# GpSimd for the state-space weight tables and the recurrence over the chunks, in a two-layer recurrent decoder step

## Chip, cores and metric

One core of a Trainium2 chip. The time is that of one execution on the device, in microseconds (us), median of the runs shown.

## What is computed

One inference step of two layers on 256 tokens of a prompt and 8 samples of 4 tokens, 288 columns in all, width 2048, float32. Only layer 0 matters here. Its input projection feeds a diagonal state-space part (S5: 64 groups, each with a complex state of 64) and a gated linear attention (GLA: 4 heads); both meet in one output projection, and an MLP follows. Cut to what the change touches:

```
abar = exp(a * dt); bbar = (abar - 1) / a * b          # complex, per group
bu   = einsum('blgq,gpq->blgp', u, bbar)               # what each token adds to the state
x[t] = abar * x[t-1] + bu[t]                           # associative_scan over the tokens
y    = Re(einsum('blgp,gqp->blgq', x, c)) + d_skip * u # then gelu and a sigmoid gate
# GLA, per head and chunk: bcum = cumsum(log_a)
qd, kd = q * exp(bcum), k * exp(-bcum)
o = tril(qd kd^T) v + qd s;  s = exp(blast) s + (k exp(blast - bcum))^T v;  o = head_rmsnorm(o) * silu(g)
```

## The kernel before

**The stream.** Every large product takes its weights in granules of 512 rows by 256 columns. SyncE loads one (`load`, L174), ScalarE rounds it to `wh` (L187), VectorE makes the rest `wl = raw - wh` (L188), and TensorE multiplies the activations with both (`mm`, L202 to L204: three products of 288 columns for each 128 x 128 block, 24 a granule). ScalarE and VectorE work one to two granules ahead; `wh` and `wl` have four buffers each, two granules.

**Work between the granules.** All else is written as generators, which `go` and `start` put on a list with a rate. After each granule `pump` adds the rate to each one's account and takes a step of it for every whole 1.0; `until` yields until a flag is set, `need` and `finish` force steps up to a flag, and `defer` puts an instruction behind a later granule. This sets only the order in which each engine's instructions stand. Each engine then goes through its own queue in that order as soon as the semaphores that it waits for allow, and an instruction that waits holds up all that stand behind it on its engine. GpSimd's queue has memsets, transfers between HBM, DRAM buffers and SBUF, and so far no arithmetic.

**S5.** Tokens go in chunks of 4, 72 chunks; pairs of groups lie on the 128 partitions (32 pairs, in 8 tables q of 4 pairs).
- `s5_tables`: `powers(q)` makes a table of abar^(3-s) bbar into `tpre`, part of the tile `hr`, two buffers (q odd and even): eight VectorE instructions, L627, L628 and twice L631 for each of two parts, and copies on ScalarE (L633). `turn(q)`, a granule later, transposes it on TensorE (L643), and `adds(q)` multiplies with the tokens (L664) into the chunks' states `eh`. `pairs` (L713 to L717, VectorE) lets every second chunk take over the state of the one before.
- `s5_scan`: 31 rounds over the remaining chunks, each a chain of three VectorE instructions (L745, L747, L748) of 128, 64 and 64 elements; two rounds a step, at rate 1.2. `last` has the samples' final states.
- `s5_y`: copies the last state (`hlast`, L785), makes the output table of c abar^(t+1) for 4 pairs (`table(q)`: L776 to L778 on VectorE, then two deferred copies by ScalarE for each of two parts, L782, into `t3`, also in `hr`, two buffers), lets the rest of the chunks take over their states (`pairs`), and multiplies on TensorE: L798, and L801, which reads `eh` and `t3`. The table of q + 1 is issued in step q.

**GLA.** `gla_decays` makes the decays (VectorE and ScalarE, rate 0.6), waits for the flag `gqk`, which is set when q and k are there, and multiplies them into q and k (L987 to L990) for heads 0 and 1, then 2 and 3. `gla_head(h)` multiplies the scores (L1019), makes the states (L1052), reads the samples' states (L1060) and gives the output (L1077 to L1085); `gla_fin` sums the squares over partitions by a product with ones (L1135). GpSimd's queue has the transfers of the samples' states (L1005, four a head) and of each head's final state (L1053).

Of the kernel before, what the change touches and what calls it, by code (L numbers as in the profile page):

```python
# [15 lines left out]
T = 288          # tokens: 256 of the prompt, then 8 samples of 4  # L16
# [4 lines left out]
KG = 4           # k-tiles of a weight granule  # L21
# [5 lines left out]
# layout of the constants' array: name -> (first column, columns)  # L27
# [49 lines left out]
class Base:  # L77
# [62 lines left out]
    def finish(self, name=None):  # L140
        """Has the side work that gives a flag (or all of it) emit what is left up to that flag."""
# [164 lines left out]
        # vectors, as columns; those of the first norm ahead of the rest  # L306
# [20 lines left out]
    def x_parts(self):  # L327
        """x for the first layer's input projections: it comes in quarters of its columns, each ahead of a granule."""
# [39 lines left out]
    def spread_r(self):  # L368
        """The tokens' scales, on all partitions."""
# [19 lines left out]
    def load_h(self):  # L389
        """x again, transposed, as the residual stream."""  # L390
# [15 lines left out]
NJ = 32          # pairs of groups  # L406
NCH = 72         # chunks: 8 of the samples, then 64 of the prompt
# [8 lines left out]
class S5:  # L416
# [59 lines left out]
    def s5_loads2(self, i):  # L476
        """More of the loads; they are spread over the first products."""
# [18 lines left out]
    def s5_tables(self):  # L496
# [7 lines left out]
        # A-bar: the states of a pair of groups on the partitions  # L504
# [51 lines left out]
        # (A-bar - 1) / a  # L556
# [15 lines left out]
        # A^8  # L572
# [5 lines left out]
        # C, block-diagonal and transposed, its imaginary part negated; B-bar  # L578
# [20 lines left out]
        # initial states of the samples  # L599
# [18 lines left out]
        def powers(q):  # L618
            """A^(3-s) B-bar of 4 pairs, block-diagonal."""
# [34 lines left out]
        def adds(q):  # L654
            """What the chunks add to the states; the kernel."""
# [49 lines left out]
    def pairs(self, q, src, dst, n, t1, t2):  # L705
        """Every second of n chunks takes over the state that the chunk before it leaves (4 pairs of groups)."""
# [12 lines left out]
    def s5_scan(self):  # L719
        v = self.nc.vector  # L720
        eh = self.eh
        self.nc.gpsimd.memset(self.hr[:, 0:2048], 0.0)
# [5 lines left out]
        def last():  # L728
            """The samples' final states."""
# [14 lines left out]
        for c in range(10, 72, 2):  # L744
            v.tensor_mul(out=t1, in0=a, in1=eh[:, :, :, c].rearrange("p (o r) j -> p o r j", o=1).to_broadcast(sh))  # L745
            next(last, None)
            v.tensor_add(out=t2, in0=t1[:, 0], in1=t1[:, 1, ::-1])  # L747
            v.tensor_add(out=eh[:, :, :, c + 2], in0=eh[:, :, :, c + 2], in1=t2)  # L748
            if c % 4 == 2:
                yield  # L750
# [1119 lines left out]
```

## Time and profile before

| | |
|---|---|
| time, three runs | 2815.69, 2812.72, 2815.59 us; median 2815.59 |
| span of the profiled execution, first to last instruction | 2813.8 us |
| the median over that span | 1.8 us |
| TensorE busy | 2778.5 us (99%) |
| VectorE, ScalarE, GpSimd busy | 1728.4, 1344.3, 212.3 us (61, 48, 8%) |
| DMA | 511.86 MB, mean 182 GB/s |

The profiled execution's own time is not listed beside its span; what lies around the span is taken as the 1.8 us to the median. How to read it: a matmul's busy time overlaps the next one's, so TensorE's share tells where it pauses, not how near it is to its peak. With TensorE at 99%, the question for a change on other engines is which of TensorE's pauses it ends, which it makes, and at what clock TensorE runs. VectorE and ScalarE matter where TensorE waits for them. Line numbers in what follows are those of the kernel before, unless the order of the changed one is shown.

### The profile page before, as it was taken

What the parts mean: (1) busy time and instruction counts of PE and PEld (TensorE: products, weight loads), DVE (VectorE), ACT (ScalarE), POOL (GpSimd) and SP (SyncE); (2) the same over time, 40 slices, a digit from 0 to 9 for tenths busy, and PEclk for the clock granted to TensorE, in tenths of its full rate; (3) what the DMA queues carried; (4) which work ended last, traced back from release to release, by engine and by line L of the source; (5) the groups of instructions that cost most, each with busy time, mean ns of one, the idle gap of its engine ahead of it and who ended that gap; (6) DMA issues with size and microseconds to landing.
All of it is one profiled execution on the core that took longest, in us unless ns stands there. A gap on an engine that the chain in (4) does not pass through costs nothing.

```text
span 2813.8 us, 52593 instructions
## 1 busy us (share of the span) xinstructions
PE 2778.5 (99%) x20648; PEld 2688.8 (96%) x20648; DVE 1728.4 (61%) x3259; ACT 1344.3 (48%) x2459; POOL 212.3 (8%) x326
## 2 busy tenths in 40 slices
PE   8999999999999999999999999999999999999998
PEld 7988999999999999999988898889999999999998
DVE  7887668555555555556466665867655555555555
ACT  5646755544444444445433343445544444444445
POOL 3110112000000000000112222210000000000000
PEclk9999999999999999999999999999999999999999
DMA  7455567555555555555678878875555555555554
GB/s 210 130 155 140 161 195 228 160 167 165 165 164 165 163 168 164 166 164 146 197 223 250 269 249 271 266 254 173 164 166 164 166 165 165 164 167 163 167 165 131
DMA packets 449511, 511.86 MB, mean 182 GB/s; under 512 B 23282, under 2 KB 423052, under 8 KB 449232
## 3 DMA queue, kind: packets, MB, share of 16 engines
q1 hardware_dynamic: 414320, 412.67, 48.6%
q0 software_dynamic: 28096, 90.16, 10.1%
q10 hardware_dynamic: 6848, 5.68, 0.6%
q8 instruction: 162, 2.65, 0.4%
q14 instruction: 85, 0.70, 0.1%
HBM read 460.08 MB, written 47.56 MB: 180 GB/s over the span
## 4 chain that ended last, share of the span: by engine, by line
PE 94%; DVE 4%; ACT 1%; issue 1%; DMA 0%; ACTq 0%; DVEq 0%
PE g L202 29%; PE g L203 28%; PE g L204 28%; PE s L1551 1%; PE n L1545 1%; PE s L1500 1%; DVE wl L188 1%; PE n L801 1%; PE s L664 0%; PE s L1419 0%; ACT wh L187 0%; DVE hr L745 0%; PE n L798 0%; PE s L1490 0%; PE s L643 0%
## 5 line engine op out<-in xcount | busy, mean ns | idle before, releaser
L187 ACT ACTIVATE wh<-raw 128x512 fp32r<-128x512 f32 x1556 | 963.1, 629 | 1203.0 <-PE g L203 1153.7
L188 DVE TENSOR_TENSOR wl<-raw,wh 128x512 fp32r<-128x512 f32 x1556 | 1035.8, 688 | 664.3 <-ACT wh L187 652.2
L202 PE MATMUL g<-xh,wh 128*128 128x288 f32 x3856 | 1158.6, 300 | 3.0 <-DVE gy L938 1.4
L204 PE MATMUL g<-xh,wl 128*128 128x288 f32 x3856 | 1138.2, 295 | 3.8 <-DVE wl L188 3.7
L203 PE MATMUL g<-xl,wh 128*128 128x288 f32 x3856 | 1141.0, 296 | 0.0
L202 PEld LDWEIGHTS g<-xh,wh 128*128 128x128 f32 x3856 | 726.4, 188 | 14.4 <-issue 9.5
L204 PEld LDWEIGHTS g<-xh,wl 128*128 128x128 f32 x3856 | 728.9, 189 | 5.4 <-DVE wl L188 5.4
L203 PEld LDWEIGHTS g<-xl,wh 128*128 128x128 f32 x3856 | 727.4, 189 | 5.2 <-issue 3.3
L203 PE MATMUL g<-hl,wh 128*128 128x288 f32 x2048 | 606.2, 296 | 0.0
L204 PE MATMUL g<-hh,wl 128*128 128x288 f32 x2048 | 605.2, 296 | 0.0
L202 PE MATMUL g<-hh,wh 128*128 128x288 f32 x2048 | 604.7, 295 | 0.0
L202 PEld LDWEIGHTS g<-hh,wh 128*128 128x128 f32 x2048 | 389.1, 190 | 0.0
L204 PEld LDWEIGHTS g<-hh,wl 128*128 128x128 f32 x2048 | 384.0, 188 | 0.0
L203 PEld LDWEIGHTS g<-hl,wh 128*128 128x128 f32 x2048 | 383.8, 187 | 0.0
L1727 DVE TENSOR_TENSOR hr<-hr,g 128x288 f32<-128x288 f32 x256 | 116.3, 454 | 186.6 <-PE g L204 186.6
L1719 ACT ACTIVATE us<-sq 128x288 f32<-128x288 f32 x128 | 56.9, 445 | 146.2 <-DVE sq L1718 146.2
L1718 DVE SCALAR_TENSOR_TENSOR sq<-g,rbc 128x288 f32<-128x288 f32 x128 | 58.5, 458 | 94.5 <-PE g L204 94.3
L1553 DVE SCALAR_TENSOR_TENSOR cin<-cin,wps,s 128x512 f32<-128x512 f32 x128 | 89.7, 742 | 7.4 <-PE s L1551 6.7
L1523 POOL DMA_DIRECT2D cin<-in_state_mlstm_c_dram x64 | 45.3, 708 | 305.6 <-DMA out_sample_mlstm_c_dram<-cin 284.0
L1334 POOL DMA_DIRECT2D out_sample_mlstm_m_dram<-mo x1 | 0.6, 620 | 838.7 <-DVE mk L1338 838.7
L1720 ACT ACTIVATE hh<-us 128x288 fp32r<-128x288 f32 x128 | 57.0, 445 | 4.1
L203 PE MATMUL g<-yl,wh 128*128 128x288 f32 x192 | 56.7, 295 | 0.0
(504 smaller groups left out, 1928.9 us busy)
## 6 DMA issues: line engine op xcount, KB each, us to landing
raw<-in_w_mlp_up_dram SPq DMA_DIRECT2D x256, 512.0 KB, 3.7
raw<-in_w_mlp_down_dram SPq DMA_DIRECT2D x256, 512.0 KB, 3.6
raw<-in_w_in_odd_dram SPq DMA_DIRECT2D x128, 512.0 KB, 4.6
raw<-in_w_in_even_dram SPq DMA_DIRECT2D x64, 512.0 KB, 4.0
cin<-in_state_mlstm_c_dram POOLq DMA_DIRECT2D x64, 512.0 KB, 5.2
out_sample_mlstm_c_dram<-cin POOLq DMA_DIRECT2D x64, 512.0 KB, 5.5
raw<-in_w_out_even_dram SPq DMA_DIRECT2D x32, 512.0 KB, 4.4
raw<-in_w_out_odd_dram SPq DMA_DIRECT2D x32, 512.0 KB, 3.6
```

Of the source, the lines that this page charges most:

```text
L187: nc.scalar.activation(out=wh[:, 0:n], in_=src, func=AF.Copy)
L188: nc.vector.tensor_tensor(out=wl[:, 0:n], in0=src, in1=wh[:, 0:n].bitcast(F32), op=ALU.subtract)
L202: nc.tensor.matmul(g.ps[j], lhsT=wh, rhs=xh, start=opens and k == 0, stop=False)
L203: nc.tensor.matmul(g.ps[j], lhsT=wh, rhs=xl, start=False, stop=False)
L204: nc.tensor.matmul(g.ps[j], lhsT=wl, rhs=xh, start=False, stop=closes and k == n - 1)
L801: nc.tensor.matmul(ps[:, j, :], lhsT=t3[:, ri, j].rearrange("p t c -> p (t c)"), rhs=eh[:, ri, jj, 0:NCH], start=False, stop=ri == 1)
L1523: nc.gpsimd.dma_start(out=cin[g], in_=part(I["state_mlstm_c"], g))
L1553: v.scalar_tensor_tensor(out=t[:, b, :], in0=t[:, b, :], scalar=wp[:, c:c + 1], in1=pb, op0=ALU.mult, op1=ALU.add)
L1718: nc.vector.scalar_tensor_tensor(out=t, in0=ps, scalar=0.0, in1=self.rbc, op0=ALU.max, op1=ALU.mult)
L1719: nc.scalar.activation(out=sq, in_=t, func=AF.Square)
L1720: nc.scalar.activation(out=hh[:, j, :], in_=sq, func=AF.Copy)
L1727: nc.vector.tensor_add(out=self.h[:, j, :], in0=self.h[:, j, :], in1=ps)
```

## The change

`powers` and the recurrence of `s5_scan` go from VectorE to GpSimd, instruction by instruction. `powers(1)` is issued at once behind `powers(0)`, and from then each table one step earlier. The output table becomes a method and goes to GpSimd, where its last instruction writes both halves into `t3` directly; ScalarE's 32 copies go. Tables 0 and 1 are issued within the recurrence, behind its 13th and 23rd round, the others two steps ahead. The end of `gla_decays` becomes a generator of its own with rate 1.0, started when k is there. `gla_fin` yields once more before its product. Comments are left out here, and so are hunks that change only them.

```diff
         def powers(q):
...
-            t = [tp.tile(sh, F32, name=f"cm{i + 1}") for i in range(2)]
+            t = [tp.tile(sh, F32, name=f"pm{i + 1}") for i in range(2)]
+            gp = nc.gpsimd
             for ri in range(2):
-                v.tensor_mul(out=t[0], in0=a[0], in1=b[ri])
-                v.tensor_mul(out=t[1], in0=a[1], in1=b[1 - ri])
+                gp.tensor_mul(out=t[0], in0=a[0], in1=b[ri])
+                gp.tensor_mul(out=t[1], in0=a[1], in1=b[1 - ri])
                 for g in range(2):
                     gs = slice(64 * g, 64 * g + 64)
-                    v.tensor_tensor(out=tpre[gs, ri, :, 0:3, g, :], in0=t[0][gs], in1=t[1][gs],
-                                    op=ALU.subtract if ri == 0 else ALU.add)
+                    gp.tensor_tensor(out=tpre[gs, ri, :, 0:3, g, :], in0=t[0][gs], in1=t[1][gs],
+                                     op=ALU.subtract if ri == 0 else ALU.add)
...
         powers(0)
+        powers(1)
         yield
         for q in range(8):
             turn(q)
-            if q < 7:
-                powers(q + 1)
+            if q < 6:
+                powers(q + 2)
...
     def s5_scan(self):
...
-        self.nc.gpsimd.memset(self.hr[:, 0:2048], 0.0)
+        gp.memset(self.hr[:, 0:2048], 0.0)
+        for g in range(2):
+            gs = slice(64 * g, 64 * g + 64)
+            self.nc.scalar.activation(out=self.cc()[gs], in_=self.ct[gs, :, :, 16 * g:16 * g + 16], func=AF.Copy)
...
         for c in range(10, 72, 2):
-            v.tensor_mul(out=t1, in0=a, in1=eh[:, :, :, c].rearrange("p (o r) j -> p o r j", o=1).to_broadcast(sh))
+            gp.tensor_mul(out=t1, in0=a, in1=eh[:, :, :, c].rearrange("p (o r) j -> p o r j", o=1).to_broadcast(sh))
             next(last, None)
-            v.tensor_add(out=t2, in0=t1[:, 0], in1=t1[:, 1, ::-1])
-            v.tensor_add(out=eh[:, :, :, c + 2], in0=eh[:, :, :, c + 2], in1=t2)
+            gp.tensor_add(out=t2, in0=t1[:, 0], in1=t1[:, 1, ::-1])
+            gp.tensor_add(out=eh[:, :, :, c + 2], in0=eh[:, :, :, c + 2], in1=t2)
+            if c in (34, 54):
+                self.table(c // 54)
             if c % 4 == 2:
                 yield
...
+    def table(self, q):
...
+        for ri in range(2):
+            gp.tensor_mul(out=tm, in0=c3[ri], in1=a3[0])
+            gp.tensor_mul(out=m3, in0=c3[1 - ri], in1=a3[1])
+            for g in range(2):
+                gs = slice(64 * g, 64 * g + 64)
+                gp.tensor_tensor(out=t3[gs, ri, :, :, 16 * g:16 * g + 16], in0=tm[gs], in1=m3[gs],
+                                 op=ALU.add if ri == 0 else ALU.subtract)
...
     def s5_y(self):
...
-                v.tensor_mul(out=tm, in0=c3[ri], in1=a3[0])
-                v.tensor_mul(out=m3, in0=c3[1 - ri], in1=a3[1])
-                v.tensor_tensor(out=tm, in0=tm, in1=m3, op=ALU.add if ri == 0 else ALU.subtract)
-                for g in range(2):
-                    gs = slice(64 * g, 64 * g + 64)
-                    self.defer(lambda t=t3[gs, ri, :, :, 16 * g:16 * g + 16], s=tm[gs]:
-                               nc.scalar.activation(out=t, in_=s, func=AF.Copy))
...
-        table(0)
         self.pairs(0, 10, 11, 31, f[0], f[1])
...
+            if q < 6:
+                self.table(q + 2)
             if q < 7:
-                table(q + 1)
                 self.pairs(q + 1, 10, 11, 31, f[0], f[1])
...
         act.activation(out=cum, in_=cum, func=AF.Exp, scale=-1.0 / 16)
-        yield from self.until("gqk")
+        self.flags.add("dec")
+
+    def gla_decays2(self):
...
+        yield from self.until("dec")
         for h in (0, 2):
...
     def gla_fin(self, h, osb, acc, r):
         nc, v = self.nc, self.nc.vector
+        yield
...
-        self.start(self.gla_decays, R_DEC, ("gla", "gb3"))
+        self.start(self.gla_decays, R_DEC, ("gla", "gb3", "dec"))
...
-        self.flag("gqk")
+        self.start(self.gla_decays2, 1.0, ("gla", "gb3"))
         self.need("tab")
```

How the change moves the instructions, at the three places that matter.

GpSimd's queue behind the memset of `kk`, from there to the transfers of the next part of u (the kernel before):

```order
L607 MEMSET kk 128x4096
L695 DMA u_dram<-us 128x288 x2
L700 DMA u_114<-u_dram 32x8x72 x4
L683 DMA kk<-kk 32x32x32
L683 DMA kk<-kk 64x32x32
```

The same place in the changed kernel:

```order
L607 MEMSET kk 128x4096
L628 ISA
L628 TENSOR_TENSOR pm_1096<-pw,bb 128x192
L629 TENSOR_TENSOR pm_1097<-pw,bb 128x192
L632 TENSOR_TENSOR hr<-pm_1096,pm_1097 64x4x3x16 x2
L628 TENSOR_TENSOR pm_1096<-pw,bb 128x192
L629 TENSOR_TENSOR pm_1097<-pw,bb 128x192
L632 TENSOR_TENSOR hr<-pm_1096,pm_1097 64x4x3x16 x2
```

The eight instructions of `powers(0)` now stand behind the memset, and ahead of them one that was not there, printed as ISA; two more tables follow before the transfers of u.

GpSimd's queue within the recurrence of the changed kernel, from its third round to its fifth (`gatt` and `s_...` are GLA's tiles):

```order
L750 TENSOR_TENSOR hr<-a_121,eh 128x128
L752 TENSOR_TENSOR hr<-hr 128x64
L753 TENSOR_TENSOR eh<-eh,hr 128x64
L895 MEMSET gatt 128x288
L1015 DMA s_2295<-in_state_gla_dram 128x2x256
L1015 DMA s_2297<-in_state_gla_dram 128x2x256
L1015 DMA s_2299<-in_state_gla_dram 128x2x256
L1015 DMA s_2301<-in_state_gla_dram 128x2x256
L750 TENSOR_TENSOR hr<-a_121,eh 128x128
L752 TENSOR_TENSOR hr<-hr 128x64
L753 TENSOR_TENSOR eh<-eh,hr 128x64
```

Before, the memset and the four transfers followed each other with no arithmetic around them. Another four transfers and one of a final state stand further on among the rounds, and so do the 16 instructions of tables 0 and 1.

VectorE's queue around `hlast`, the kernel before:

```order
L745 TENSOR_TENSOR hr<-a_121,eh 128x128 [waits DVE_49]
L747 TENSOR_TENSOR hr<-hr 128x64 [waits DVE_49]
L748 TENSOR_TENSOR eh<-eh,hr 128x64 [waits DVE_49]
L188 TENSOR_TENSOR wl<-raw,wh 128x512 [waits DMAHW4_49,PE_49,Activation_49]
L188 TENSOR_TENSOR wl<-raw,wh 128x512 [waits PE_49,Activation_49]
L785 COPY hlast<-eh 128x64 [waits DVE_49]
L188 TENSOR_TENSOR wl<-raw,wh 128x512 [waits DMAHW5_49,PE_49,Activation_49]
L188 TENSOR_TENSOR wl<-raw,wh 128x512 [waits PE_49,Activation_49]
L776 TENSOR_TENSOR hr<-hr,pw 128x256
```

And the changed kernel:

```order
L789 COPY hlast<-eh 128x64 [waits Pool_49]
L188 TENSOR_TENSOR wl<-raw,wh 128x512 [waits DMAHW5_49,PE_49,Activation_49]
L188 TENSOR_TENSOR wl<-raw,wh 128x512 [waits PE_49,Activation_49]
L715 TENSOR_TENSOR hr<-pw,eh 128x8x31
L716 TENSOR_TENSOR hr<-a4i,eh 128x8x31
L718 TENSOR_TENSOR hr<-hr 128x8x31 [waits DVE_49]
L719 TENSOR_TENSOR eh<-eh,hr 128x2x4x31 [waits DVE_49]
```

The copy now waits for GpSimd, in front of the casts of one granule and of `pairs(0)` (L715 to L719); the rounds ahead of it and the table's six instructions behind the casts are gone.

## Rows read from the trace of the kernel before

**Rows 1.** The page: busy time of each engine, share, instructions

```profile
PE 2778.5 (99%) x20648; PEld 2688.8 (96%) x20648; DVE 1728.4 (61%) x3259; ACT 1344.3 (48%) x2459; POOL 212.3 (8%) x326
```

**Rows 2.** Stretches: start:end, length, then busy us (and instructions) of each engine, clock, DMA

```profile
200.00:225.00 25.00, 23.56 (x183) 21.98 (x182) 23.41 (x62) 14.31 (x29) 3.39 (x5) 1.00 0.60 173
...
425.00:450.00 25.00, 25.00 (x191) 25.00 (x190) 19.17 (x42) 11.79 (x21) 4.98 (x7) 1.00 0.76 245
```

**Rows 3.** Waits of TensorE from 75 to 500 us: total us, times, longest

```profile
PE n L801 <- ACT hr L782: 3.4, 2, 3.0
PE g L204 <- DVE wl L188: 2.7, 4, 1.1
PE s L1019 <- DVE gkk L990: 2.0, 1, 2.0
PE n L801 <- DVE eh L717: 1.6, 1, 1.6
PE s L1135 <- DVE sqa L1085: 1.5, 2, 1.1
PE g L202 <- DVE gy L938: 1.4, 1, 1.4
PE s L398 <- ACT hr L399: 1.1, 1, 1.1
PE g L202 <- DVE gq L906: 0.9, 1, 0.9
PE s L643 <- DVE hr L631: 0.9, 1, 0.9
```

**Rows 4.** Stretches of the page's clock below 1.00 (the column after POOL)

```profile
237.07:240.48 3.41, 3.41 (x17) 3.41 (x17) 3.31 (x10) 0.41 (x1) 0.55 (x1) 0.50 0.66 198
281.44:288.27 6.83, 6.83 (x33) 6.83 (x32) 2.60 (x8) 0.50 (x2) 0.00 (x0) 0.50 0.28 75
```

**Rows 5.** TensorE in order of time (start, length): the first L801 of the output

```profile
235.49 0.64 PE L801 MATMUL n<-eh,hr 128*128 128x72 f32 x4 [1.62 <-DVE eh L717]
```

**Rows 6.** VectorE's groups, 60 to 520 us: busy us, mean ns, then idle before

```profile
L745 DVE TENSOR_TENSOR hr<-a,eh 128x128 f32<-128x128 f32 x31 | 12.5, 402 | 0.6
...
L748 DVE TENSOR_TENSOR eh<-eh,hr 128x64 f32<-128x64 f32 x31 | 8.7, 282 | 1.1
...
L747 DVE TENSOR_TENSOR hr<-hr 128x64 f32<-128x64 f32 x31 | 6.9, 223 | 0.8
```

**Rows 7.** The stretch of the recurrence on VectorE

```profile
168.00:225.00 57.00, 52.05 (x389) 49.26 (x388) 53.95 (x146) 28.93 (x60) 6.53 (x10) 1.00 0.57 162
```

**Rows 8.** GpSimd in order of time: the memset of kk; two of the start

```profile
77.63 3.54 POOL L607 MEMSET kk<- 128x4096 f32 x1
...
8.96 0.36 POOL L875 MEMSET sacc<- 128x288 f32 x1
9.37 0.10 POOL L876 MEMSET sacc<- 128x2 f32 x1
```

**Rows 9.** VectorE in order of time: powers(0), pairs(7), hlast, first output table

```profile
83.69 0.72 DVE L631 TENSOR_TENSOR hr<-cm,cm 64x192 f32<-64x192 f32 x2
...
167.63 0.43 DVE L717 TENSOR_TENSOR eh<-eh,cm 128x256 f32<-128x256 f32 x1
...
230.10 0.21 DVE L785 COPY hlast<-eh 128x64 f32<-128x64 f32 x1
...
231.43 0.42 DVE L776 TENSOR_TENSOR hr<-hr,pw 128x256 f32<-128x256 f32 x1
...
233.69 0.41 DVE L713 TENSOR_TENSOR hr<-pw,eh 128x248 f32<-128x248 f32 x1
```

**Rows 10.** ScalarE's groups, 60 to 300 us: a load of a function table

```profile
L954 ACT ACT_TABLE_LOAD x1 | 1.3, 1283 | 0.0
```

**Rows 11.** Transfers by issuing queue: number, KB each, us to landing

```profile
bi<-in_mlstm_b_i_dram POOLq DMA_DIRECT2D x1, 0.0 KB, 4.5
```

**Rows 12.** GpSimd's groups, 60 to 240 us: a transfer for the first heads

```profile
L1005 POOL DMA_DIRECT2D s<-in_state_gla_dram x8 | 5.7, 712 | 0.0
```

More of the change, by code (lines that the diff above doesn't have):

```diff
@@ L744, in s5_scan, with cc, t3_of @@
         for c in range(10, 72, 2):
-            v.tensor_mul(out=t1, in0=a, in1=eh[:, :, :, c].rearrange("p (o r) j -> p o r j", o=1).to_broadcast(sh))
+            gp.tensor_mul(out=t1, in0=a, in1=eh[:, :, :, c].rearrange("p (o r) j -> p o r j", o=1).to_broadcast(sh))
             next(last, None)
-            v.tensor_add(out=t2, in0=t1[:, 0], in1=t1[:, 1, ::-1])
-            v.tensor_add(out=eh[:, :, :, c + 2], in0=eh[:, :, :, c + 2], in1=t2)
+            gp.tensor_add(out=t2, in0=t1[:, 0], in1=t1[:, 1, ::-1])
+            gp.tensor_add(out=eh[:, :, :, c + 2], in0=eh[:, :, :, c + 2], in1=t2)
+            if c in (34, 54):
+                self.table(c // 54)
             if c % 4 == 2:
                 yield
+    def cc(self):
+        return self.hr[:, 2560:3584].rearrange("p (r j q) -> p r j q", r=2, j=NJ)
+    def t3_of(self, q):
+        return self.hr[:, 1024 * (q % 2):1024 * (q % 2) + 1024].rearrange("p (r j t c) -> p r j t c", r=2, j=4, t=4)
+    def table(self, q):
+        gp = self.nc.gpsimd
+        js = slice(4 * q, 4 * q + 4)
+        sh = [128, 4, 4, 16]
+        t3, cc = self.t3_of(q), self.cc()
+        tm, m3 = (self.hr[:, o:o + 256].rearrange("p (j t q) -> p j t q", j=4, t=4) for o in (2048, 2304))
+        c3 = [cc[:, ri, js, :].rearrange("p j (o c) -> p j o c", o=1).to_broadcast(sh) for ri in range(2)]
+        a3 = [self.pw[:, ri, js, :].rearrange("p j (t o) -> p j t o", o=1).to_broadcast(sh) for ri in range(2)]
+        for ri in range(2):
[5 more added lines that the diff above has]
+                                 op=ALU.add if ri == 0 else ALU.subtract)
     def s5_y(self):
@@ L755, in s5_y @@
         eh, es, hr = self.eh, self.es, self.hr
-        tms, m3s = ([hr[:, o:o + 256].rearrange("p (j t q) -> p j t q", j=4, t=4) for o in os]
-                    for os in ((2048, 2304), (4096, 4352)))
-        cc = hr[:, 2560:3584].rearrange("p (r j q) -> p r j q", r=2, j=NJ)
         f = [hr[:, o:o + 256].rearrange("p (r j n) -> p r j n", r=2, j=4) for o in (3584, 3840)]
-        for g in range(2):
-            gs = slice(64 * g, 64 * g + 64)
-            nc.scalar.activation(out=cc[gs], in_=self.ct[gs, :, :, 16 * g:16 * g + 16], func=AF.Copy)
-        sh = [128, 4, 4, 16]
-        def t3_of(q):
-            return hr[:, 1024 * (q % 2):1024 * (q % 2) + 1024].rearrange("p (r j t c) -> p r j t c", r=2, j=4, t=4)
-        def table(q):
-            js = slice(4 * q, 4 * q + 4)
-            t3 = t3_of(q)
-            c3 = [cc[:, ri, js, :].rearrange("p j (o c) -> p j o c", o=1).to_broadcast(sh) for ri in range(2)]
-            a3 = [self.pw[:, ri, js, :].rearrange("p j (t o) -> p j t o", o=1).to_broadcast(sh) for ri in range(2)]
-            for ri in range(2):
-                tm, m3 = tms[ri], m3s[ri]
-                v.tensor_mul(out=tm, in0=c3[ri], in1=a3[0])
-                v.tensor_mul(out=m3, in0=c3[1 - ri], in1=a3[1])
-                v.tensor_tensor(out=tm, in0=tm, in1=m3, op=ALU.add if ri == 0 else ALU.subtract)
-                for g in range(2):
-                    gs = slice(64 * g, 64 * g + 64)
-                    self.defer(lambda t=t3[gs, ri, :, :, 16 * g:16 * g + 16], s=tm[gs]:
-                               nc.scalar.activation(out=t, in_=s, func=AF.Copy))
         self.load_h_part(4)
@@ L792, in s5_y @@
             js = slice(4 * q, 4 * q + 4)
-            t3 = t3_of(q)
+            t3 = self.t3_of(q)
             y4 = self.u4[:, js, :]
```

4 lines of the change are left out of this document (3 added, 1 removed).

## Prediction

> **What bounds the kernel now.** I began with the page. TensorE is busy for 2778.5 of 2813.8 us [rows 1], so no change elsewhere can bring more than TensorE's own pauses. The stretches say where those lie: from 200 to 225 us TensorE is busy for 23.56 of 25.00 us beside a VectorE at 23.41, and from 425 to 450 us, out of reach of this change, it is busy throughout [rows 2]. The reader is to see that the first layer, from 75 to some 375 us, is the one place where VectorE is full and TensorE pauses.
>
> Then the list of waits, cut to 75 to 500 us, which names each pause and what ended it [rows 3]. TensorE stands for 3.4 us before L801 until ScalarE has copied the output table (L782), for 1.6 us before the same line until VectorE's `pairs` (L717) is done, and for 2.7, 2.0, 1.5, 1.4 and 0.9 us until VectorE gives it split weights, decayed keys, squares, and two evacuated accumulators. A last 0.9 us, before L643, is for the weight table of `powers`. All of these queue behind work that the change takes off VectorE and ScalarE.
>
> Third, the granted clock. It is 0.50, the lower level (1.2 GHz), for 3.41 us from 237.07 us and for 6.83 us from 281.44 us, each shortly after a pause of TensorE before L801 [rows 4, 5]. At half the clock about half of such a stretch is lost: 1.7 and 3.4 us, together 5.1 us.
>
> **What the change takes away.** VectorE loses 64 instructions of `powers`, 93 of the recurrence and 48 of the output table; ScalarE loses that table's 32 copies. One round of the recurrence costs VectorE 0.40 + 0.22 + 0.28 us [rows 6]; with 31 rounds that is 28 us out of the 57 us from 168 to 225 us, of which VectorE is busy 53.95 [rows 7]. So there the backlog goes. I let seven waits fall: 3.4 + 2.7 + 2.0 + 1.6 + 1.5 + 1.4 + 0.9 = 13.5 us [rows 3]. The 1.5 us before L1135 falls also because `gla_fin` now sends its product one granule later, and the 2.0 us before L1019 because VectorE no longer has the recurrence ahead of the decayed keys; the order moves those and their use one granule forward together, so pacing alone would not free them. With the two pauses before L801 gone, I take both stretches of half clock back: 5.1 us. Together 18.6 us. The 1.1 us before L398 stays, and I give the later end of `gla_fin` no cost: its last split stands behind the 74th pair of casts and is used two products later.
>
> **What GpSimd's work costs.** The trace has no GpSimd instruction that reads SBUF, so its price is bounded. From below: VectorE's rows for the same shapes. From above: the writes of GpSimd's memsets, 3.54 us for 4096 elements and 0.36 us for 288 [rows 8], thus 0.84 ns an element and 0.1 us fixed; if two reads and a write went one after another at that pace, 64, 128, 192 and 256 elements would take 0.26, 0.42, 0.58 and 0.75 us. A memset that waits for the one before starts 0.05 us after its end (9.37 against 8.96 + 0.36) [rows 8]. I take the upper prices, since they are GpSimd's own rows.
>
> *First place, the turn of table 0.* TensorE already waits there, so each delay counts in full. GpSimd's memset of `kk` ends at 77.63 + 3.54 = 81.17 us [rows 8], and `powers(0)` stands behind it. Eight instructions of 0.58 us and four waits make 4.84 us, to 86.0 us, where VectorE was done at 83.69 + 0.72 = 84.41 [rows 9]: 1.6 us later (with VectorE's prices, 0.36 us each or 2.9 us in all, 0.3 us earlier). Between the two the order shows one instruction that was not there, printed as ISA: a reload of GpSimd's library of code. No row has it. From below it is nothing. The nearest rows are ScalarE's load of a function table, 1283 ns, and a GpSimd transfer of next to no bytes, 4.5 us to landing [rows 10, 11]; code has to be fetched, so I take 4.5. TensorE then stands 6.1 us longer, and I add one short stretch of half clock, 1.7 us: 7.8 us.
>
> The Trainium skill (GPSIMD Engine Reference, 2.1 Instruction dispatch) says that the first call into a freshly loaded library pays about 6 us. By that the delay would be 7.6 us in place of 6.1; no run here shows it yet.
>
> `powers(1)` to `powers(7)`, 4.8 us each, are issued a table ahead, and a table spans two granules on TensorE, of 24 products each; at 191 products in 25 us [rows 2] that is 6.3 us without the small products. The six transfers of `u` that now stand behind `powers(2)` feed tables 6 and 7 alone. No cost.
>
> *Second place, the copy of `hlast`.* VectorE is in order, and `hlast` (L785, now L789) waits for GpSimd's last round; queued behind it are the casts of a granule and `pairs(0)`, for which TensorE waits at L801. So GpSimd has a due time. TensorE reached L801 at 235.49 - 1.62 = 233.87 us [rows 5]; without the waits in between (2.0, 1.4, and 2.5 of the casts' 2.7 us) that is 228.0. From `hlast` at 230.10 to the restart at 235.49 VectorE took 5.4 us, less 2.3 us (231.43 to 233.69) for a table that is no longer there [rows 9]: 3.1 us. So GpSimd is due at 224.9, and it may begin when pairs(7) ends at 167.63 + 0.43 [rows 9]: 56.8 us. It has to do 31 rounds of 0.42 + 0.26 + 0.26 + 0.15 = 1.09 us (33.8 us), two tables of 6.2 us (each eight instructions of 0.75 us and four waits), nine transfers at 0.71 us [rows 12] (6.4 us), and a memset of 0.4 us: 53.0 us. It is in time by 3.8 us, and would be up to 1.22 us a round. With VectorE's prices it has over 10 us to spare. In its queue stand also transfers that wait for TensorE and VectorE in the first head; the rows place these only roughly, and a wait there comes off the same margin. So no cost, but the cover is thin: past 1.22 us, each 0.1 us more in a round puts 3.1 us on TensorE.
>
> In the output stage a table of 6.2 us is issued two steps ahead of its use, and a step has at least one granule, 3.1 us, and its own small products: no cost.
>
> **Sum.** 18.6 - 7.8 = 10.8 us. The profiled execution's span of 2813.8 us becomes 2803.0; the median of the runs, 2815.6, lies 1.8 us above that span, so **2804.8 us**.
>
> **Rivals.**
> *The reload costs nothing* (it runs under the memset, or the library is there already). For it: no row prices it. Against it: it stands behind the memset in one queue. TensorE then loses 1.6 us at most: 18.6 - 1.6 = 17.0, thus 2798.6 us, or 2797 at VectorE's prices.
>
> *GpSimd is a few us late at `hlast`.* For it: the margin is 3.8 us on a sum of 53, and the smallest instructions may have a larger fixed part than a memset. Five us late, with the short stretch of half clock, gives 2804.8 + 6.7 = 2811.5 us: no difference that can be told.
>
> *GpSimd and VectorE shut each other out*, the rival on the other side. If a GpSimd instruction that reads and a VectorE instruction of two inputs from SBUF can't run together, their times add. From 168 to 225 us VectorE keeps, of the 29 rounds that lie in it, 53.95 - 29 x 0.90 = 27.8 us [rows 6, 7], nearly all of that kind; GpSimd's rounds and tables, without waits and transfers, are 31 x 0.94 + 2 x 6.0 = 41.1. Together 68.9 us against 56.8: GpSimd is 12 us late, VectorE stands at `hlast`, TensorE at L801 with a long stretch of half clock (3.4 us): 2804.8 + 15.5 = 2820.3 us; with the small gaps not shared, up to 2828. It turns the result once a round costs over 1.5 us. For it: VectorE's two-input casts run in every granule. Against it: no row here has both at once.
> This is the Trainium skill's rule (SBUF - State Buffer, "Who interferes with whom"): the later of the two fully blocks. No run here shows it yet.
>
> *The change does not do what it says* can be left out: the order shows the instructions on GpSimd, in number and place.
>
> **How the numbers follow.** Forecast 0.38; reload free 0.15; a few us late 0.25; shut out 0.22. What this kernel's measurement can tell from no change is some 0.2%, 5.6 us: faster is below 2810.0, slower above 2821.2. The first two cases and the lower edge of the third are faster, 0.57; the rest of the third and the lower part of the fourth the same, 0.25; the rest slower, 0.18. The range goes from the free reload at VectorE's prices, 2796, into the fourth case, 2823; what it leaves out is the worse half of that case.
>
> **What would show it.** Right: VectorE's busy time falls by some 70 us; the waits of L801 on `hr` and `eh` and of L1019 are gone; before the first transposes of `hr` TensorE stands for 5 to 8 us on GpSimd; `hlast` waits for nothing; a round on GpSimd takes 1.0 to 1.2 us. Wrong: a wait of several us before L801 that ends with VectorE's `pairs`, behind a `hlast` that waited for GpSimd; rounds of 1.5 us and more; casts on VectorE that take longer beside GpSimd than in granules without it; or no wait before the first transposes, which would mean that the reload is free.

## The result, and the profile after

The changed kernel takes 2834.73 us, median of 4 runs (2830.83 to 2838.55), beside 2815.64 us for 4 runs of the kernel before: a ratio of 1.0072, 95% interval 1.006 to 1.0083. It is 19.1 us slower where 10.8 us faster were forecast. The profiled execution is the slowest of the four, 2838.55 us with a span of 2836.5, which is 22.7 us more than the span of before.

The page, the line that answers to [rows 1] (busy us of each engine, share, instructions):

```profile
PE 2784.7 (98%) x20648; PEld 2695.7 (95%) x20648; DVE 1690.6 (60%) x3054; ACT 1332.4 (47%) x2427; POOL 354.9 (13%) x547
```

VectorE's busy time fell by 1728.4 - 1690.6 = 37.8 us, not by some 70. The waits of TensorE from 75 to 500 us, which answer to [rows 3]:

```profile
PE n L804 <- DVE eh L719: 22.6, 2, 20.5
PE s L659 <- DVE hr L652: 2.9, 1, 2.9
PE s L644 <- POOL hr L632: 2.3, 2, 2.0
PE g L202 <- ACT sq L1194: 1.7, 1, 1.7
...
PE g L204 <- DVE wl L188: 0.5, 1, 0.5
```

Most of the waits that I let fall did fall: those on ScalarE's copy of the output table, on `gkk`, on `gy` and before the product with ones are gone, and that for split weights is down to 0.5 us. In their place stand 22.6 us before L804 (L801 of before), 2.9 us at the turn of table 3, and 1.7 us on a sigmoid of ScalarE. The one long wait has its source on VectorE (in order of time: start, length, and in brackets the idle time before and what ended it):

```profile
253.92 0.22 DVE L789 COPY hlast<-eh 128x64 f32<-128x64 f32 x1 [20.06 <-POOL eh L753]
```

That is the second place of the prediction: `hlast`, with the casts and `pairs(0)` queued behind it, stood for 20.06 us until GpSimd had done its last round. The stretches of half clock (the granted clock is the column after POOL, TensorE's busy time the first one after the length) answer to [rows 4]:

```profile
85.34:92.17 6.83, 6.43 (x38) 5.69 (x39) 2.55 (x6) 6.76 (x12) 6.32 (x11) 0.50 0.27 77
126.30:133.13 6.83, 6.20 (x28) 6.23 (x29) 3.34 (x7) 2.27 (x6) 1.46 (x2) 0.50 0.39 106
238.94:266.25 27.31, 9.21 (x41) 9.24 (x42) 8.87 (x17) 1.04 (x2) 20.89 (x42) 0.50 0.24 82
303.79:310.62 6.83, 6.83 (x33) 6.83 (x32) 2.89 (x7) 1.04 (x2) 4.04 (x7) 0.50 0.30 79
395.95:399.37 3.42, 3.42 (x17) 3.42 (x16) 0.69 (x1) 0.63 (x1) 0.00 (x0) 0.50 0.45 153
```

In the third TensorE stands until 257.05 us, where half the clock costs nothing, and then works for 9.2 us at half clock. At half the time that TensorE works in it (an estimate), the stretches cost 3.2, 3.1, 4.6, 3.4 and 1.7 us, together 16.0 us. The kernel before has the last one too, at 373.60 us, and with the two of [rows 4] it loses 6.8 us so. Half clock thus makes some 9 of the 22.7 us; the waits grew from 15.9 to 31.5 us, by the two lists from 75 to 500 us.

Where the time goes can be read from when TensorE begins the same weight granule (the first product, L202, of each, but the second of granule 48, which stands behind the wait of before for `wl`) in the two traces; this is worked out from the two lists of instructions:

| granule | before, us | after, us | after later by | what lies between |
|---|---|---|---|---|
| 0 | 13.75 | 14.09 | 0.3 | |
| 16 | 80.21 | 79.72 | -0.5 | |
| 18 | 91.12 | 95.20 | 4.1 | turn of table 0, half clock |
| 25 | 126.88 | 136.47 | 9.6 | turn of table 3, half clock |
| 37 | 177.87 | 188.44 | 10.6 | |
| 48 | 229.87 | 232.59 | 2.7 | VectorE without the recurrence |
| 50 | 243.88 | 268.10 | 24.2 | `hlast`, half clock |

So 8 us were won beside the recurrence, as meant, some 10 lost at the weight tables (4.6 and 5.5), where I had 7.8 at the turn of table 0 and nothing at the others, and 21 at `hlast`, where I had nothing. Some 3 of the 10 us belong to this execution alone: up to granule 36 the kernels of experiments 1, 3, 4 and 8 have the same instructions, and in their traces the weight tables cost 6.7 to 7.1 us, with stretches of half clock of 3.41 us in place of 6.83.

### The profile page after: what moved, and what is told of

The parts are those of the page before. It is cut to its first block, busy times and chain, and to the rows that moved or that the text cites. A ratio compares the mean times of both kernels' runs of the same rounds, so it can differ in the third digit from the quotient of the medians.

```text
span 2836.5 us, 52620 instructions
## 1 busy us (share of the span) xinstructions
PE 2784.7 (98%) x20648; PEld 2695.7 (95%) x20648; DVE 1690.6 (60%) x3054; ACT 1332.4 (47%) x2427; POOL 354.9 (13%) x547
## 3 DMA queue, kind: packets, MB, share of 16 engines
q8 instruction: 162, 2.65, 0.4%
## 4 chain that ended last, share of the span: by engine, by line
PE 92%; DVE 1%; POOL 1%; ACT 1%; issue 1%; DVEq 0%; ACTq 0%
PE g L202 28%; PE g L203 28%; PE g L204 28%; PE s L1562 1%; PE n L1556 1%; PE s L1511 1%; PE n L804 1%; DVE wl L188 0%; PE s L1430 0%; PE s L665 0%; PE s L1501 0%; PE n L801 0%; ACT wh L187 0%; POOL hr L750 0%; PE s L1439 0%
## 5 line engine op out<-in xcount | busy, mean ns | idle before, releaser
L202 PE MATMUL g<-xh,wh 128*128 128x288 f32 x3856 | 1160.6, 301 | 1.1 <-DVE gq L910 0.4
L202 PEld LDWEIGHTS g<-xh,wh 128*128 128x128 f32 x3856 | 728.1, 189 | 12.6 <-issue 7.6
L202 PE MATMUL g<-hh,wh 128*128 128x288 f32 x2048 | 604.7, 295 | 0.0
L202 PEld LDWEIGHTS g<-hh,wh 128*128 128x128 f32 x2048 | 389.1, 190 | 0.0
L1566 POOL DMA_DIRECT2D out_sample_mlstm_c_dram<-cin x64 | 46.1, 720 | 98.3 <-DVE cin L1564 96.7
```

The source lines that it names most:

```text
L202: nc.tensor.matmul(g.ps[j], lhsT=wh, rhs=xh, start=opens and k == 0, stop=False)
L1566: nc.gpsimd.dma_start(out=part(O["sample_mlstm_c"], g), in_=t)
```

## Experiments

Each kernel ran on one chip together with the kernel before; the differences of medians below are to those runs.

**1. The recurrence back on VectorE.**

```diff
-            gp.tensor_mul(out=t1, in0=a, in1=eh[:, :, :, c].rearrange("p (o r) j -> p o r j", o=1).to_broadcast(sh))
+            v.tensor_mul(out=t1, in0=a, in1=eh[:, :, :, c].rearrange("p (o r) j -> p o r j", o=1).to_broadcast(sh))
             next(last, None)
-            gp.tensor_add(out=t2, in0=t1[:, 0], in1=t1[:, 1, ::-1])
-            gp.tensor_add(out=eh[:, :, :, c + 2], in0=eh[:, :, :, c + 2], in1=t2)
+            v.tensor_add(out=t2, in0=t1[:, 0], in1=t1[:, 1, ::-1])
+            v.tensor_add(out=eh[:, :, :, c + 2], in0=eh[:, :, :, c + 2], in1=t2)
```

> The changed kernel with the 31 rounds of the recurrence back on VectorE; both weight tables stay on GpSimd. Theory (GpSimd is too slow for the recurrence, its own instructions being dear and VectorE's two-input instructions taking turns with them): hlast waits for nothing, the 20.5 us of TensorE before L804 fall below 3 us, the waits of 2.0 and 2.9 us at the first tables stay, and some 4 of the 8 us won between 188 and 230 us are given back to VectorE's backlog: 2834.7 - 21.5 + 4 = 2817 us (2812 to 2822). Rival (VectorE's own queue, not GpSimd, makes pairs(0) late): more than 10 us of the wait at L804 stay, 2826 us or more.

Measured: 2819.75 us beside 2814.81, ratio 1.002 (1.001 to 1.003). TensorE's waits:

```profile
PE g L204 <- DVE wl L188: 5.5, 4, 2.4
PE n L804 <- DVE eh L719: 3.2, 2, 2.1
...
PE s L659 <- DVE hr L652: 2.2, 1, 2.2
```

`hlast` waits for nothing. The wait before L804 falls to 3.2 us, a little over what was expected, the two at the turns stay (2.3 us before L644, and L659), and VectorE's backlog is back in the 5.5 us for split weights. So GpSimd in the recurrence makes about three quarters of the loss (14.2 of 19.1 us), and what is left of the change is still slower than before.

**2. The recurrence alone on GpSimd**, in the kernel before, tables and pace untouched: the three lines of experiment 1 the other way round.

> The kernel before with the recurrence alone on GpSimd; both tables on VectorE, pace as before. Theory (a due time: only what GpSimd is late by counts): rounds of 1.8 us and 6.4 us of transfers, without the two tables amid them, make 63 us from pairs(7) to hlast, where VectorE comes to hlast after some 53 us; hlast is copied at about 231 to 232 us, as against 230.1 before, TensorE stands some 10 us before L801 but comes there about 8 us earlier, and a longer stretch of half clock costs 2 to 3 us: 2817 to 2821 us. Rival (the parts add up: the whole change less its other parts leaves 14 us for the recurrence): 2827 to 2831 us.

Measured: 2818.16 us beside 2814.37, ratio 1.0012 (1.0003 to 1.002), the median of 12, one of which took 3747.72 us. The waits of TensorE, and `hlast`:

```profile
PE n L801 <- DVE eh L717: 11.8, 1, 11.8
```

```profile
232.91 0.22 DVE L785 COPY hlast<-eh 128x64 f32<-128x64 f32 x1 [11.32 <-POOL eh L748]
```

As the due time has it: `hlast` is copied at 232.91 us, 2.8 us later than before [rows 9], since TensorE and VectorE came 7 us earlier and then stood. The parts don't add up: by the medians the recurrence costs 3.8 us alone, and 19.1 - 4.9 = 14.2 us in the change (with it and without it). There two tables of GpSimd, 12.6 us, stand amid the rounds, and its work from the first round to the last takes 76.1 us; here it takes 64.5 us.

**3. VectorE's casts beside the recurrence left out.** This separates the price of a round from the turns that it takes with VectorE's casts. `ncast` counts the granules; LO and HI take in the 12 beside the recurrence.

```diff
-            wl = self.wl_p.tile([128, KG, 128], F32R, name="wl")
...
+            out = LO <= self.ncast < HI
+            wl = None if out else self.wl_p.tile([128, KG, 128], F32R, name="wl")
             nc.scalar.activation(out=wh[:, 0:n], in_=src, func=AF.Copy)
+            if out:
+                wl = wh
+            else:
+                nc.vector.tensor_tensor(out=wl[:, 0:n], in0=src, in1=wh[:, 0:n].bitcast(F32), op=ALU.subtract)
```

> The changed kernel without VectorE's two splits of the weights in the 12 granules that lie beside the recurrence; TensorE takes the rounded weights in their place, so as many products are made. Theory (instructions of VectorE and GpSimd with two inputs from SBUF take turns): a round takes 1.42 to 1.5 us, as it does in the changed kernel while VectorE stands, the recurrence with its two tables 62 to 66 us in place of 76, hlast waits for 6 to 11 us in place of 20, 2819 to 2826 us. Rival (a round is dear by itself, or through the transfers): rounds stay at 1.8 us or more on the mean, hlast waits for 17 us or more, 2832 us or more.

Measured: 2825.11 us in one run. GpSimd's groups, first of the changed kernel, then of this one (busy us, mean ns of one | idle before), and this kernel's `hlast`:

```profile
L750 POOL TENSOR_TENSOR hr<-a,eh 128x128 f32<-128x128 f32 x31 | 21.0, 676 | 4.1 <-DVE eh L719 1.9
L753 POOL TENSOR_TENSOR eh<-eh,hr 128x64 f32<-128x64 f32 x31 | 14.7, 474 | 2.4
```

```profile
L757 POOL TENSOR_TENSOR hr<-a,eh 128x128 f32<-128x128 f32 x31 | 17.7, 569 | 4.1 <-DVE eh L726 1.9
L760 POOL TENSOR_TENSOR eh<-eh,hr 128x64 f32<-128x64 f32 x31 | 12.0, 387 | 2.4
```

```profile
DVE hlast L796 <- POOL eh L760: 10.2, 1, 10.2
```

The lines are seven further down. With the third of its kind (455 and 341 ns) a round's instructions fall from 676 + 474 + 455 = 1605 ns to 569 + 387 + 341 = 1297 ns, with the small pauses between them from 1.83 to 1.53 us on the mean (1.42 where nothing else runs), a little over the 1.42 to 1.5 of the theory, and `hlast`'s wait falls from 20.1 to 10.2 us. Nothing was changed on GpSimd. So about half of its lateness was the doing of VectorE's casts. The other half is in the main the plain price of a round: what a round still has over 1.42 us makes 31 x 0.11 = 3.4 us.

**4. The same casts with one input in place of two**: `tensor_copy(out=wl, in_=src)` in those 12 granules.

> The changed kernel in which VectorE, in the 12 granules beside the recurrence, copies the raw weights in place of subtracting: one input from SBUF in place of two, so the results are not the reference's there, and the number of instructions is the same. Theory (only instructions with two inputs from SBUF take turns): the copies take the same time beside GpSimd as without it, a round 1.42 to 1.5 us, hlast waits for 6 to 11 us, 2819 to 2827 us. Rival (every VectorE instruction of this size shuts GpSimd out): rounds of 1.7 us or more, hlast waits for 15 us or more, 2830 us or more.

Measured: 2830.83 us in one run; `hlast` waits for 13.5 us, outside the theory's range and short of the rival's, while the time is just within the rival's. Two rows of VectorE in order of time, and GpSimd's groups:

```profile
178.53 1.25 DVE L192 CAST wl<-raw 128x512 fp32r<-128x512 f32 x2
...
194.71 0.43 DVE L192 CAST wl<-raw 128x512 fp32r<-128x512 f32 x1 [1.71 <-PE g L210]
```

```profile
L756 POOL TENSOR_TENSOR hr<-a,eh 128x128 f32<-128x128 f32 x31 | 18.6, 600 | 4.1 <-DVE eh L725 1.9
```

A copy that starts together with a GpSimd instruction takes 0.43 us, and that instruction (64 elements, 0.35 us alone) takes 0.67 us; two copies that each start within one take 1.25 us together. GpSimd's three instructions of a round take 600 + 425 + 346 = 1371 ns, between the 1297 without casts and the 1605 with subtractions. So my theory was too narrow: these copies take turns with GpSimd as well. That GpSimd loses less fits a copy being shorter than a subtraction (0.43 against 0.69 us); no run sets the two lengths apart from the number of inputs.

**5. `powers` back on VectorE, and 6. `powers` alone on GpSimd.** In 5, `gp = v` in `powers` of the changed kernel; in 6 the part of the diff on `powers`, in the kernel before.

> The changed kernel with powers back on VectorE, still issued two tables ahead; recurrence and output tables stay on GpSimd. Theory (GpSimd's powers stretch VectorE's casts and pairs by taking turns, and so make the turns of tables 0 and 3 late): the waits of 2.0 us before L644 and 2.9 us before L659 and the stretches of half clock at 85 and 126 us go, the recurrence starts 8 to 10 us earlier and ends as much earlier, hlast still waits for about 20 us: 2826 us (2822 to 2830). Rival (the powers' work is the same burden on VectorE's own queue): the recurrence starts less than 3 us earlier, 2831 to 2836 us.

> The kernel before with powers alone on GpSimd, issued two tables ahead. Theory (beside GpSimd's powers VectorE's pairs and casts take turns and come late at the turn of a table): waits of about 2 us before the first transposes of hr on GpSimd and of 2 to 3 us before the transposes of kt on VectorE, each with a stretch of half clock; the granules around 130 us are 6 to 9 us later than before, and as VectorE's backlog by 225 us is no smaller, the loss stays: 2820 to 2825 us. Rival (VectorE's freed 20 us repay it later): 2812 to 2817 us.

Measured: 5 takes 2827.17 us beside 2814.81, 1.0039 (1.0025 to 1.0053); 6 takes 2819.92 beside 2814.58, 1.0022 (1.0013 to 1.0031). Their waits of TensorE, 5 first:

```profile
PE n L804 <- DVE eh L719: 22.6, 2, 20.4
```

```profile
PE s L644 <- POOL hr L632: 2.3, 2, 2.0
PE s L659 <- DVE hr L652: 2.2, 1, 2.2
```

With `powers` on VectorE the waits on GpSimd before the turn of table 0 and on VectorE before L659 are gone, and `hlast` still waits for 20.1 us: its due time moved with it. Alone, `powers` brings both waits and 5.3 us, just under the 2820 us of the theory; by the granules 3.2 us come at the turn of table 0, with 3.41 us of half clock, and 1.9 us at that of table 3, where no half clock followed. GpSimd's powers cost, 6.7 us in company (19.1 - 12.4) and 5.3 alone.

**7. The pace alone, and 8. all but the pace.** In 7, `gla_decays2` and the further step in `gla_fin`, in the kernel before; in 8 the changed kernel without them.

> The kernel before with the two changes of pace alone (the end of gla_decays as a generator of its own with rate 1.0, one more step in gla_fin); nothing on GpSimd. Theory (the gain of 8 us between 188 and 230 us came from VectorE's freed time, not from the pace): the 1.5 us before L1135 go and little else, 2812 to 2816 us. Rival (the pace alone brings it): the waits before L1019 and of the split weights go too, 2805 to 2809 us.

> The changed kernel with the pace of before (no generator of its own for the end of gla_decays, no further step in gla_fin). Theory (hlast's wait sets the time, and the pace only moves a wait of 1.5 us from L1135 to one on ScalarE's sigmoid): the wait of some 20 us at L804 stays, the 1.7 us on ScalarE go and 1.5 us before the product with ones come back: 2830 to 2836 us. Rival (the later order of the decays is what fills VectorE's and GpSimd's time during the recurrence): hlast waits for less than 16 us, under 2829 us.

Measured: 7 takes 2818.27 us beside 2814.81, 1.0013 (1.0004 to 1.0022); 8 takes 2827.09 beside 2814.58, 1.0045 (1.0032 to 1.0059). 7 came out where neither theory nor rival had it. 8 lies below its theory, in the time of its rival, but `hlast` does not wait for less than 16 us, as the rival had it. In 7:

```profile
PE n L801 <- DVE eh L717: 3.3, 1, 3.3
PE g L202 <- ACT sq L1189: 1.7, 1, 1.7
```

The 1.5 us before L1135 are gone, but 1.7 us on ScalarE's sigmoid stand in their place, the wait before L801 on VectorE has grown from 1.6 to 3.3 us, and the 2.0 us for the decayed keys are still 1.7. So the pace moves the waits and frees nothing on balance; it was no part of the gain. In 8, `hlast` still waits, for 21.5 us, yet the time is 19.1 - 12.5 = 6.6 us under the change's:

```profile
PE n L804 <- DVE eh L719: 19.6, 1, 19.6
```

```profile
290.00:310.00 20.00, 20.00 (x169) 19.12 (x167) 15.77 (x26) 11.86 (x25) 13.35 (x18) 1.00 0.45 116
```

One wait before L804 in place of two (19.6 against 22.6), none on the sigmoid (1.7), and full clock, here and from 375 to 400 us, where the change has two stretches at half (3.4 + 1.7): 9.8 us, less 1.9 us that are back before the product with ones. That makes 7.9 us, by which the two traces also drift apart behind granule 48. In all they lie 11.0 us apart, with 3 us at the weight tables, where the instructions are the same; that the medians lie only 6.6 us apart fits the profiled execution of the change being its slowest.

**9. The output table alone on GpSimd, 10. the same with tables 0 and 1 later, 11. nothing on GpSimd.** 9 is the kernel before with the method `table` and its calls, 10 issues table 0 behind the 29th round and table 1 behind `hlast`. 11 leaves the table on VectorE and changes one thing in it:

```diff
-                v.tensor_tensor(out=tm, in0=tm, in1=m3, op=ALU.add if ri == 0 else ALU.subtract)
                 for g in range(2):
                     gs = slice(64 * g, 64 * g + 64)
-                    self.defer(lambda t=t3[gs, ri, :, :, 16 * g:16 * g + 16], s=tm[gs]:
-                               nc.scalar.activation(out=t, in_=s, func=AF.Copy))
+                    v.tensor_tensor(out=t3[gs, ri, :, :, 16 * g:16 * g + 16], in0=tm[gs], in1=m3[gs],
+                                    op=ALU.add if ri == 0 else ALU.subtract)
```

> The kernel before with the output table alone on GpSimd (tables 0 and 1 issued behind rounds 13 and 23 of VectorE's recurrence, the others two steps ahead, both halves written at once, ScalarE's 32 copies gone); powers, recurrence and pace as before. Theory (a part pays where GpSimd has slack at its use): TensorE's 3.4 us before L801 on ScalarE's copy and about 1.6 us on pairs(0) go, with the 1.7 us of half clock behind them; VectorE's pairs(1) to pairs(7) get up to 0.3 us longer where tables run beside them, hidden: 2808 to 2812 us. Rival (taking turns with pairs and casts gives it back): the wait before L801 turns to one on VectorE of 3 us or more, 2813 to 2819 us.

> The output table alone on GpSimd as in the run of that name, but table 0 behind the 29th round and table 1 behind hlast, in place of the 13th and 23rd. Theory (two tables amid VectorE's recurrence cost the casts 3 to 5 us by taking turns): the 5.9 us of waits for split weights fall back to about 3, the waits before L801 stay under 3 us: 2808 to 2811 us. Rival (the turns taken are the same wherever the tables stand): 2811 to 2814 us, with a wait of 2 us or more before the first L801.

> The kernel before with nothing on GpSimd; VectorE writes both halves of the output table into t3 itself (two instructions of 64 partitions for each part in place of one and two copies by ScalarE). Theory (what the output tables gain on GpSimd is ScalarE's copies and the order, not VectorE's time): TensorE's 3.4 us before L801 on ScalarE's copy and the 3.4 us of half clock behind it go, VectorE's 0.8 us more in a table lengthen the wait before the first L801 by some 1 us: 2808 to 2811 us. Rival (the copies' wait only turns into one on VectorE's pairs): 2813 to 2817 us.

Measured: 9 takes 2811.49 us beside 2814.58, 0.999 (0.9981 to 0.9999); 10 takes 2811.75 beside 2814.39, 0.9989 (0.998 to 0.9998); 11 takes 2810.03 beside 2814.39, 0.9988 (0.9979 to 0.9996). Waits of TensorE in 9, 10 and 11, in this order:

```profile
PE g L204 <- DVE wl L188: 5.9, 6, 2.4
```

```profile
PE s L1139 <- DVE sqa L1089: 4.2, 3, 2.3
```

```profile
PE n L800 <- DVE eh L717: 3.7, 2, 2.6
```

In all three the 3.4 us on ScalarE's copy are gone, and with them the stretch of half clock at 281 us. In 9 and 10 the waits for split weights (2.7 us before, 5.9 in 9, 4.1 in 10) and before the product with ones (1.5 before, 2.9 in 9, 4.2 in 10) grow, wherever tables 0 and 1 stand: what 10 was to bring it didn't, and its time is in the rival's range, though without the wait before L801 that the rival had. In 11 GpSimd does no arithmetic at all, and the gain is as large; the price is 3.7 us before L800 in place of 1.6. So the one part of the change that pays does so by the copies that it drops, not by GpSimd. By the medians 11 is faster than both kernels, 4.4 us under the one before.

What VectorE gets back is on the page. The groups of the output table in the kernel before, 60 to 520 us:

```profile
L778 DVE TENSOR_TENSOR hr<-hr 128x256 f32<-128x256 f32 x16 | 6.8, 425 | 0.5
L776 DVE TENSOR_TENSOR hr<-hr,pw 128x256 f32<-128x256 f32 x16 | 6.7, 418 | 0.0
L777 DVE TENSOR_TENSOR hr<-hr,pw 128x256 f32<-128x256 f32 x16 | 6.7, 417 | 0.0
```

The busy lines of 9 and 6:

```profile
PE 2775.3 (99%) x20648; PEld 2685.2 (96%) x20648; DVE 1726.7 (61%) x3211; ACT 1332.3 (47%) x2427; POOL 262.3 (9%) x390
```

```profile
PE 2780.1 (99%) x20648; PEld 2690.3 (95%) x20648; DVE 1717.4 (61%) x3195; ACT 1344.9 (48%) x2459; POOL 257.2 (9%) x390
```

In 9, 6.8 + 6.7 + 6.7 = 20.2 us of instructions left VectorE, and its busy time fell by 1728.4 - 1726.7 = 1.7 us. In 6, 64 instructions of 0.35 us left, 22.6 us, and it fell by 11.0. In the whole change 22.6 + 28.1 + 20.2 = 70.9 us left, 37.8 came off. Nearly all of the rest went into longer instructions on VectorE: its casts, for one, take 0.84 us on the mean where they overlap with an arithmetic instruction of GpSimd (45 casts from 75 to 260 us in the trace of the change) and 0.69 us where they don't (25 casts).

## Why the prediction was wrong

**The step that failed first is the price of a round on GpSimd**, 1.09 us worked out from memsets. The changed kernel's rows, one round beside a working VectorE and one while VectorE stands at `hlast`:

```profile
198.99 0.85 POOL L750 TENSOR_TENSOR hr<-a,eh 128x128 f32<-128x128 f32 x1
199.93 0.32 POOL L752 TENSOR_TENSOR hr<-hr 128x64 f32<-128x64 f32 x1
200.33 0.82 POOL L753 TENSOR_TENSOR eh<-eh,hr 128x64 f32<-128x64 f32 x1
...
244.03 0.52 POOL L750 TENSOR_TENSOR hr<-a,eh 128x128 f32<-128x128 f32 x1
244.62 0.32 POOL L752 TENSOR_TENSOR hr<-hr 128x64 f32<-128x64 f32 x1
245.02 0.35 POOL L753 TENSOR_TENSOR eh<-eh,hr 128x64 f32<-128x64 f32 x1
245.44 0.52 POOL L750 TENSOR_TENSOR hr<-a,eh 128x128 f32<-128x128 f32 x1
```

Alone a round takes 0.52 + 0.32 + 0.35 us with pauses of 0.07 to 0.08, and the next begins 245.44 - 244.03 = 1.41 us after it. The prices of the longer instructions were about right, or high: 0.51 us for 192 elements (0.58 taken), 0.62 for 256 (0.75 taken). Those of the short ones were low: 0.32 to 0.35 for 64 (0.26 taken), 0.52 for 128 (0.42 taken). By the rows for 64 and 256 elements some 0.22 us are fixed and 1.6 ns an element are added (an estimate), where the prediction had 0.1 us and 2.5 ns from memsets.

**The step that failed second is the case**: "shut out" was the mechanism, and I gave it 0.22. VectorE and GpSimd in turns, where a weight table is made beside `pairs` (VectorE, then GpSimd):

```profile
123.62 0.73 DVE L715 TENSOR_TENSOR cm<-pw,eh 128x256 f32<-128x256 f32 x1
124.28 0.73 DVE L716 TENSOR_TENSOR cm<-a4i,eh 128x256 f32<-128x256 f32 x1
125.04 0.69 DVE L718 TENSOR_TENSOR cm<-cm,cm 128x256 f32<-128x256 f32 x1
...
126.39 0.24 DVE L651 COPY hr<-s 128x96 f32<-128x96 f32 x1
126.55 0.23 DVE L652 SCALAR_TENSOR_TENSOR hr<-cst,cols,s 128x32 f32<-128x32 f32 x1
```

```profile
123.23 0.84 POOL L628 TENSOR_TENSOR pm<-pw,bb 128x192 f32<-128x192 f32 x1
124.04 0.69 POOL L629 TENSOR_TENSOR pm<-pw,bb 128x192 f32<-128x192 f32 x1
```

The ends alternate: GpSimd's at 124.07, VectorE's at 124.35, GpSimd's at 124.73, VectorE's at 125.01. Each of `pairs`'s instructions takes 0.69 to 0.73 us, where its last takes 0.43 alone [rows 9]; the copy and the last instruction, which read PSUM, take 0.24 and 0.23 beside GpSimd, where their means before were 0.25 and 0.24. The turns are not always one for one: from 193.67 to 195.88 us VectorE ran an addition of `last` and three casts one behind the other, and GpSimd's instruction stood through all four.

```profile
193.62 2.65 POOL L750 TENSOR_TENSOR hr<-a,eh 128x128 f32<-128x128 f32 x1
```

The Trainium skill's rule (SBUF - State Buffer, "Who interferes with whom") is that a VectorE instruction with two inputs from SBUF, or one in its fast two-port copy mode, and a GpSimd instruction that reads SBUF hold a shared port in turns, the later one blocked for as long as the other lasts. These rows and experiment 3 agree with it for two inputs. The copies of experiment 4 also take turns; that they ran in the two-port mode no row says.

**The due time held.** From the end of pairs(7) at 177.6 us VectorE came to `hlast` at 253.92 - 20.06 = 233.9: 56.2 us, where the prediction had 56.8. What GpSimd had to do in that time was 53.0 us in the prediction and 76.1 in the trace (177.78 to 253.89). Of the 23 us, the transfers, the memset and the tables carry nothing: 2.93 + 0.61 + 2.91 us of transfers against 6.4, and tables of 7.0 and 5.6 us against 6.2 each. All of it lies in the rounds, 56.7 us or 1.83 a round, against 33.8: 31 x 0.33 = 10 us is the price alone, and 31 x 0.41 = 13 us the turns. Either would have put GpSimd past the due time; the threshold of 1.22 us a round stood in the prediction, and 1.42 is over it without any rival. The rival "shut out" ended at 2820 to 2828 us because it kept the low price of a round and let the turns cost GpSimd alone.

**"No cost" for `powers(1)` to `powers(7)` was wrong.** I asked whether GpSimd would be in time for each table, and it was: table 0 took 5.0 us (4.84 taken), the next five 5.4 to 7.1 us. What came late was VectorE: casts and `pairs` in turns with GpSimd, and behind them the copy of `kt` (L651, L652), for which TensorE stood 2.9 us before L659, with a stretch of half clock behind that. From granule 18 to 25 this is 5.5 us; in experiment 6, without the half clock, it is 1.9 us.

**The first place, the turn of table 0, came out smaller, for a wrong reason.** GpSimd's rows there, with VectorE's cast beside them:

```profile
77.03 3.55 POOL L607 MEMSET kk<- 128x4096 f32 x1
80.45 0.69 DVE L188 TENSOR_TENSOR wl<-raw,wh 128x512 fp32r<-128x512 f32 x1 [0.91 <-ACT wh L187]
80.67 0.85 POOL L628 TENSOR_TENSOR pm<-pw,bb 128x192 f32<-128x192 f32 x1
81.49 0.51 POOL L629 TENSOR_TENSOR pm<-pw,bb 128x192 f32<-128x192 f32 x1
```

The memset ends at 80.58 and the first multiplication begins at 80.67, so the reload between them has 0.1 us, not 4.5. The first call runs 0.85 us in place of 0.51, but VectorE's cast ran until 81.14, so this is a turn with it. In experiment 9 the first arithmetic of GpSimd, here behind transfers that end at 171.40, takes 0.65 us in place of 0.62:

```profile
171.54 0.65 POOL L774 TENSOR_TENSOR hr<-hr,pw 128x256 f32<-128x256 f32 x1
```

The rival "reload free" was right on this term. The Trainium skill's 6 us for the first call after a load (GPSIMD Engine Reference, 2.1 Instruction dispatch) doesn't show here. What was right is the slower work (1.6 us forecast; 2.3 us waited against 0.9) and that a stretch of half clock follows: of 6.83 us in this trace, at a cost of 3.2 us, and of 3.41 us in those of experiments 1, 3, 4 and 8, at the 1.7 us forecast. By the granules the place costs 4.6 us here and 3.2 to 3.7 us there, against 7.8.

**The gains** were mostly real where TensorE could use them: waits of 3.4, 2.2, 2.0, 1.4 and 1.5 us [rows 3] are gone or smaller. Three terms failed: the 1.6 us before L801 on `pairs`, which became the long wait; the 1.5 us before L1135, which came back as 1.7 on the sigmoid (experiment 7); and the 5.1 us of clock, since half clock follows the new pauses too and costs an estimated 16.0 us in place of 6.8. And the instructions that left VectorE's queue were paid for in longer ones that stayed, which the prediction nowhere counted.

Open: why the later pace brings the wait on the sigmoid and the stretches of half clock behind it was not tried, nor why the same pause is followed by 6.83 us of half clock in one trace and 3.41 us in others, nor whether a place among the rounds exists where a table's turns are free.

## What to carry to other kernels

Work of two SBUF operands that went from VectorE to GpSimd here did not free VectorE for as long as it had taken there: count GpSimd's instructions as time in which VectorE's own such instructions can't run, and see which queue that makes late, also where GpSimd itself is in time. A chain of short dependent instructions was dear on GpSimd: a round took 1.42 us there with nothing beside it, 0.90 us on VectorE. If such a chain must end before a copy that an in-order engine has ahead of its other work, compare its length with the due time at a price taken from short instructions, and first look whether the gain doesn't lie in something simpler that the same edit does, as the 32 dropped copies here.

## What the runs showed of the hardware

- GpSimd's tensor_tensor in float32, alone: 0.32 to 0.35 us for 64 elements a partition, 0.52 for 128, 0.51 for 192, 0.62 for 256 (0.59 and 0.72 for 192 and 256 in the tables' last instructions, on 64 partitions), and 0.07 to 0.08 us between dependent ones.
- VectorE's one-input copies of 128x512 from SBUF take turns with GpSimd too (two of them 1.25 us, one that begins with GpSimd's 0.43); its two instructions that read PSUM beside GpSimd didn't (0.25 and 0.24 us on the mean, in the change as before).
- Moving 20.2 us of instructions off VectorE lowered its busy time by 1.7 us.
- Where GpSimd's first arithmetic came, behind a reload of its library, the pause was 0.1 us, and the first instruction took 0.65 us in place of 0.62 (experiment 9).
- One GpSimd instruction of 0.52 us stood for 2.65 us behind four VectorE instructions that followed each other.
